# A hybrid retention/HGRN2 decoder layer: four mixing groups first, then three feed-forward groups, nearly all products by a seven-product scheme

## The chip, the cores and the metric

One NeuronCore of a Trainium2 chip runs the whole program. TensorE (PE) multiplies matrices into PSUM; its weight loads are shown as PEld. VectorE (DVE), ScalarE (ACT) and GpSimd (POOL) do elementwise work; SyncE (SP) issues the transfers, which 16 DMA engines carry. The metric is the device time of the program in microseconds (us), as the median of the runs; lower is better.

## What is computed

One layer of a decoder over 2048 prompt tokens and 8 samples of 8 tokens (2112 in all), in float32, with width 1024 and a hidden width of 4096:

```
h = rmsnorm(x, norm_mix_w)
rq, rk, rv, rg, hq, hf, hi, hg = split(h @ w_in, 8)        # 8 parts of 4 heads x 128
o_r = retention(rotary(rq), rotary(rk), rv)                # state S <- g S + k^T v, decay g per head
f = lb + (1 - lb) * sigmoid(hf)
o_h = hgrn2(silu(hq), 1 - f, hi, log f)                    # state S <- diag(f) S + k^T v
o = [head_rmsnorm(o_r) * silu(rg), head_rmsnorm(o_h) * silu(hg)]
x = x + o @ w_out
x = x + square(relu(rmsnorm(x, norm_ffn_w) @ w_up)) @ w_down
y = rmsnorm(x, final_norm_w)
```

The prompt starts from zero states, the samples from given ones. The outputs are y for both and the final states. The two recurrences run over the tokens in order, in chunks of 128 tokens here.

## The kernel before

Activations lie with channels on the 128 partitions and tokens along the free axis. A product of two float32 matrices is made of three TensorE products of rounded parts: each operand is cut in a high part `hi` (a cast on ScalarE) and the rest `lo` (a subtraction on VectorE or GpSimd), and hi*hi + hi*lo + lo*hi are summed in PSUM. So each block of 128 x 128 weights costs three products, each as wide as the tokens that move through it, and a weight tile `raw` of 128 x 1024 is loaded, cast (L277) and subtracted (`second_part`, L292) ahead of its use (`weight`, L252).

The tokens go in three groups: 512 of the prompt; the 64 of the samples and 768 of the prompt; 768 of the prompt. Each goes through the whole layer before the next. Within a group, `mix` (L614) loops over four heads p: `project` (L665) makes six blocks of the input projection through `proj` (L339, products at L352), in pieces of at most 512 tokens, `values` (L708) the two value parts with tokens as the stationary operand (L728), and `mixer` (L829) plans the recurrence: decays in logarithms, scores in chunks on TensorE, states, gates. `residual` (L1181) and `out_proj` (L1345) make the output projection and add x.

The feed-forward of the first group is plain (`up_first`, `down_first`). The other two groups use a scheme of seven products in place of eight for a product of 2 x 2 blocks: sums S1 to S4 of weight quarters A11 to A22 and T1 to T4 of activation quarters B11 to B22 are operands beside the quarters (`PRODUCTS`, `OCTET`), each product is half the group's tokens wide, and results are added on the way out of PSUM (`up`, L1492; `down`, L1579; products at L1176). The weight sums are made once on VectorE while the first group's feed-forward and the second's mixing run (`plan_sums`, L1314), written to DRAM and loaded in both later groups. Input weights are also cut once and kept in DRAM as hi and lo.

The order of the work is written by an agenda that counts ticks: one tick for each step of three products in `proj`, or for two products elsewhere (`tick`, L221). Functions are due at a tick (`later`, `at`), so mixer work is laid between wide products; `side` is a second list, for `plan_sums`. A scheduler then orders each engine's instructions by readiness, with the order of the program as priority, and the engines take their queues in order. Slabs (42 of 832 columns) are the working tiles in SBUF; a tile is used again when its last reader is done. All weight loads go out through SP's queue.

PSUM is split in two tiles of two banks for projections (`pj`) and four of one bank (`mm`).

Of the kernel before, what the change touches and what calls it, by code (L numbers as in the profile page):

```python
# [15 lines left out]
P = 128  # L16
# [12 lines left out]
SLAB = 832  # L29
NSLAB = 42  # L30
NLD = 6
# [5 lines left out]
GROUPS = ((0, 0, 512), (NS, 512, 768), (0, 1280, 768))  # L37
NT = NS + SEQ
WT = 1024
N_IN, N_OUT, N_UP, N_DN = 32, 8, 32, 32  # L40
W_OUT0 = N_IN
W_UP0 = W_OUT0 + N_OUT
W_DN0 = W_UP0 + N_UP
NQ = FF // (4 * P)
NO = NQ // 2

W_UQ0 = W_DN0 + N_DN
W_DQ0 = W_UQ0 + N_UP
NW = W_DQ0 + N_DN

N_MADE = 4

# [10 lines left out]
PLACE = {name: q for q, name in QUARTER.items()}  # L63
# [17 lines left out]
N_ORDER = (0, 1, 4, 5, 2, 3, 6, 7)  # L81

# [63 lines left out]
def in_blocks():  # L146
    for p in range(H):
        if p:
            yield from ((7, p - 1), (3, p - 1))
        yield from ((5, p), (4, p), (0, p), (1, p), ("v", p))  # L150
    yield from ((7, H - 1), (3, H - 1))


def lay_out_weights(w_in, w_out, w_up, w_down):
    w = np.empty((NW, P, WT), np.float32)
    wi = w_in.reshape(KB, P, 8, H, DK)
    i = 0
    for part, p in in_blocks():
        if part != "v":
            w[i] = wi[:, :, part, p].transpose(1, 0, 2).reshape(P, WT)  # L160
            i += 1
            continue
# [6 lines left out]
    for ps in (range(0, H - 1), range(H - 1, H)):  # L169
        bl = [wo[kind, p, :, n] for n in N_ORDER for p in ps for kind in (1, 0)]  # L170
        for j in range(0, len(bl), 8):
            w[i] = np.stack(bl[j:j + 8], 1).reshape(P, WT)
            i += 1
    wu = w_up.reshape(KB, P, FF // P, P)
    for f in range(FF // P):
        w[i] = wu[:, :, f].transpose(1, 0, 2).reshape(P, WT)
        i += 1
    wd = w_down.reshape(8, 4, P, 4, 256)
    for f in range(8):
        for n in range(4):  # L180
            w[i] = wd[f, :, :, n].transpose(1, 0, 2).reshape(P, WT)
            i += 1
# [25 lines left out]
class Kernel:  # L208
# [12 lines left out]
    def tick(self):  # L221
# [4 lines left out]
        self.n_ticks += 1  # L226
        while self.side and self.side[0][0] <= self.n_ticks:
            self.side.popleft()[1]()
# [8 lines left out]
    def get(self, dt=F32):  # L237
        return self.sl.tile([P, SLAB], dt, tag="slab", name="slab")
# [6 lines left out]
    def load(self):  # L245
        return self.ld.tile([P, SLAB], F32, tag="ld", name="ld")
# [5 lines left out]
    def weight(self, i):  # L252
        n = len(self.stream)
        while self.w_next < min(i + 1 + self.ahead, n):
            j = self.w_next
            e = self.stream[j]
            if e[0] == "p":

                self.wts[j] = tuple(self.wp.tile([P, WT], F32R, tag=tag, name=tag) for tag in ("hi", "lo"))
                for part, kept in zip(self.wts[j], self.kept[e[1]]):  # L260
                    self.nc.sync.dma_start(part.bitcast(F32), kept)
                self.w_next += 1
                self.w_load = max(self.w_load, j + 1)
                continue
            while self.w_load <= j or j >= self.n_first and self.w_load <= j + 2 and self.w_load < n:
                if self.stream[self.w_load][0] == "p":
                    break
                k, later = self.w_load, self.w_load >= self.n_first
                raw = self.raws[k] = self.wp.tile([P, WT], F32, tag="sum" if later and k % 3 else "raw", name="raw",
                                                  bufs=4 if later and k % 3 else 2)  # L270
                e = self.stream[k]
# [1532 lines left out]
```

## Time and profile before

| | |
|---|---|
| runs | 2559.78, 2559.78, 2560.04 us; median 2559.78 |
| profiled execution | span 2557.8 us from the first instruction to the last, 2.0 us under the median of the runs |
| TensorE busy | 2527.3 us, 99%, 14681 products |
| VectorE, ScalarE, GpSimd busy | 67%, 46%, 28% |
| moved by DMA | 443 MB, 173 GB/s on the mean |

A row of instruction groups has the line, the engine, the operation, out<-in with shapes, the count, then busy time and the mean of one in ns, then the idle time of the engine before them and what ended it. Mean durations of products overlap each other, since they are pipelined: a pace has to be taken from counts over a stretch. A row of stages has the stretch, its length, and for each engine its busy time and count, then the clock granted to TensorE as a share, the DMA share and GB/s.

### The profile page before, as it was taken

The numbers are of one execution on the slowest core, as the hardware profiler recorded it, in microseconds if no ns is written. First come the engines' busy times: TensorE is split into PE (matmuls) and PEld (weight loads), VectorE is DVE, ScalarE is ACT, GpSimd is POOL, SyncE is SP. The second block draws the span as 40 slices with busy tenths as digits, with TensorE's granted clock in tenths as the row PEclk, the third lists the DMA queues.
The fourth block names the chain that finished last, engine by engine and source line by source line (L and its number), as shares of the span: only waits on it lengthen the run. The fifth ranks groups of instructions, "written<-read, shape, count | busy, mean of one in ns | idle before, by whom it ended". The sixth has DMA issues, their size and how long they took to land. (4 is left out here: it accounts for less than half of the span.)

```text
span 2557.8 us, 37262 instructions
## 1 busy us (share of the span) xinstructions
PE 2527.3 (99%) x14681; PEld 2398.5 (94%) x14681; DVE 1702.4 (67%) x2165; ACT 1172.3 (46%) x1591; POOL 704.8 (28%) x453
## 2 busy tenths in 40 slices
PE   8999999999999999999999999999999999999997
PEld 7888888888999999999999999999999999999997
DVE  6777775556667667664656978775456465559886
ACT  6776532325444444344434544544445264344443
POOL 4333241111324243101222322243134012223222
PEclk9999999999999999999999999999999999999999
DMA  7666854563264564634457545342223325565552
GB/s 265 219 220 223 294 197 172 190 215 125 94 231 152 198 205 173 230 126 165 166 171 258 191 173 170 129 165 93 94 100 112 120 91 179 176 226 186 176 179 83
DMA packets 147391, 443.13 MB, mean 173 GB/s; under 512 B 15120, under 2 KB 37392, under 8 KB 147216
## 3 DMA queue, kind: packets, MB, share of 16 engines
q1 hardware_dynamic: 147072, 440.73, 49.8%
q8 instruction: 116, 1.90, 0.3%
q14 instruction: 59, 0.48, 0.1%
q10 hardware_dynamic: 144, 0.02, 0.0%
HBM read 331.11 MB, written 108.79 MB: 172 GB/s over the span
## 5 line engine op out<-in xcount | busy, mean ns | idle before, releaser
L352 PE MATMUL pj<-slab,hi 128*128 128x416 f32 (+2 forms) x2844 | 739.3, 363 | 7.4 <-ACT hi L277 6.3
L277 ACT CAST hi<-raw 128x1024 fp32r<-128x1024 f32 x330 | 347.7, 1054 | 673.4 <-PE pu L1176 191.5
L352 PEld LDWEIGHTS pj<-slab,hi 128*128 128x128 f32 x2844 | 513.0, 189 | 38.7 <-ACT hi L277 6.3
L292 POOL TENSOR_TENSOR lo<-raw,hi 128x1024 fp32r<-128x1024 f32 x92 | 248.0, 2695 | 849.6 <-ACT hi L277 788.9
L1176 PE MATMUL pd<-slab,hi 128*128 128x416 f32 (+1 forms) x1792 | 469.4, 342 | 5.1 <-DVE slab L1619 3.1
L292 DVE TENSOR_TENSOR lo<-raw,hi 128x1024 fp32r<-128x1024 f32 x238 | 302.0, 1269 | 199.1 <-ACT hi L277 198.6
L352 PE MATMUL pj<-slab,lo 128*128 128x416 f32 (+2 forms) x1422 | 433.6, 363 | 0.0
L1176 PE MATMUL pu<-slab,hi 128*128 128x416 f32 (+1 forms) x1600 | 408.3, 342 | 0.0
L1176 PEld LDWEIGHTS pd<-slab,hi 128*128 128x128 f32 x1792 | 329.6, 188 | 8.7 <-DVE slab L1619 3.7
L1176 PE MATMUL pd<-slab,lo 128*128 128x416 f32 (+1 forms) x896 | 307.8, 344 | 0.0
L1176 PEld LDWEIGHTS pu<-slab,hi 128*128 128x128 f32 x1600 | 294.0, 188 | 1.5
L352 PEld LDWEIGHTS pj<-slab,lo 128*128 128x128 f32 x1422 | 259.5, 188 | 15.4 <-DVE lo L292 0.8
L1176 PE MATMUL pu<-slab,lo 128*128 128x416 f32 (+1 forms) x800 | 264.2, 343 | 0.0
L352 PE MATMUL mm<-slab,hi 128*128 128x512 f32 x740 | 229.6, 390 | 0.0
L728 PE MATMUL pjv<-hi,slab 128*128 128x256 f32 x1088 | 212.4, 287 | 1.3 <-ACT slab L738 1.3
L1375 DVE TENSOR_TENSOR slab<-slab 128x832 fp32r<-128x832 f32 (+1 forms) x144 | 163.0, 1149 | 36.9 <-ACT slab L1371 17.4
L728 PEld LDWEIGHTS pjv<-hi,slab 128*128 128x128 f32 x1088 | 174.3, 190 | 3.7 <-ACT slab L738 2.2
L1371 ACT CAST slab<-slab 128x832 fp32r<-128x832 f32 (+1 forms) x144 | 122.4, 862 | 116.2 <-DVE slab L1382 83.2
L1176 PEld LDWEIGHTS pd<-slab,lo 128*128 128x128 f32 x896 | 168.1, 188 | 0.5
L352 PEld LDWEIGHTS mm<-slab,hi 128*128 128x128 f32 x740 | 138.5, 188 | 29.2 <-ACT slab L1206 0.4
L728 PE MATMUL pjv<-lo,slab 128*128 128x256 f32 x544 | 153.8, 283 | 0.0
L1176 PEld LDWEIGHTS pu<-slab,lo 128*128 128x128 f32 x800 | 149.7, 188 | 0.5
(214 smaller groups left out, 3685.8 us busy)
## 6 DMA issues: line engine op xcount, KB each, us to landing
raw<-w SPq DMA_DIRECT2D x270, 512.0 KB, 4.2
u<-ld SPq DMA_DIRECT2D x32, 416.0 KB, 4.5
slab<-u SPq DMA_DIRECT2D x32, 416.0 KB, 5.6
u<-ld SPq DMA_DIRECT2D x32, 384.0 KB, 4.5
slab<-u SPq DMA_DIRECT2D x32, 384.0 KB, 5.7
ld<-x SPq DMA_DIRECT2D x16, 416.0 KB, 6.1
ld<-x SPq DMA_DIRECT2D x16, 384.0 KB, 4.1
raw<-su1S SPq DMA_DIRECT2D x8, 512.0 KB, 4.3
```

Source lines behind the costliest of these rows:

```text
L277: self.nc.scalar.copy(hi, raw)
L292: eng.tensor_tensor(out=lo, in0=self.second.pop(j), in1=hi.bitcast(F32), op=ALU.subtract)
L352: self.nc.tensor.matmul(pj[:, i, :T2], w, a[:, c0:c1], start=j == 0 and q == 0, stop=j == n - 1 and q == 2)
L728: nc.tensor.matmul(pj[:, i * 256:(i + 1) * 256], a[:, s:s + C], ww, start=kb == 0 and q == 0, stop=kb == KB - 1 and q == 2)
L1176: self.nc.tensor.matmul(*a, **k)
L1371: self.nc.scalar.copy(hi[:, :g.T], B[name][:, :g.T])
L1375: self.nc.vector.tensor_tensor(out=lo[:, :g.T], in0=B[name][:, :g.T], in1=hi.bitcast(F32)[:, :g.T], op=ALU.subtract)
```

## The change

All four groups' mixing runs first, in groups of 512, 512, 512 and 576 tokens (the samples are with the last one). Then the feed-forward runs in three groups of 704, cut without regard to the mixing groups.

- Six of the eight parts of the input projection come as three pairs of parts a head (`PAIRS`). The pairs of the first head are plain in all groups, those of the second head in the first group; the rest takes seven products of half the group's tokens (`two`). Weights come as half units of 512 columns with hi and lo in one tile. Sums are made on GpSimd in the first group that needs them, kept in DRAM as hi and lo and loaded later; raw quarters are loaded and cut anew in each group, their low part on GpSimd. The activations are normalised before the projection, not after it, go through DRAM (`g.td`), and their sums T1 to T4 are made in `plan_sides`.
- Sigmoids of a head are gathered, with one pair of table loads. The score tiles `AT`, `ATs` exist twice, for even and odd heads.
- The output projection is cut in two halves: heads 0 and 1 while mixing (`out_part`), with x added and the result sent to DRAM; heads 2 and 3 at the start of a feed group (`out_proj`). All head outputs go to DRAM (`spill`) and come back (`load_heads`), gathered from the mixing groups that hold the tokens.
- The feed-forward is by seven products throughout. The four weight sums of a set are made on GpSimd for each group (`first_sums`, `last_sum`), in 16 raw tiles; nothing of them is kept. The reciprocal of the mean square in `scale_residual` goes; `guard` adds a term to the last norm in its place.
- The pools are opened one after the other: 62 slabs of 576 columns and eight PSUM tiles of one bank while mixing, then 44 slabs of 704 and four PSUM tiles of two banks.
- A tick is now 704 columns moved through TensorE (`TICK`).

The core of the diff:

```diff
-GROUPS = ((0, 0, 512), (NS, 512, 768), (0, 1280, 768))
+GROUPS = ((0, 0, 512), (0, 512, 512), (0, 1024, 512), (NS, 1536, 512))
+NFG = 3
+NRAW, NSUM, NFRAW = 4, 2, 16
+POOL_PARTS = ("A12", "S1", "S4")
+PAIRS = ((5, 4), (0, 1), (7, 3))
+PLAIN = (0, 1, 2) if STRASSEN_IN else tuple(range(NBP))
+LATE = (3, 4, 5)
+BP_ORDER = (("A11", "B11"), ("S2", "T2"), ("S3", "T3"), ("S1", "T1"), ("A12", "B21"), ("A22", "T4"), ("S4", "B22"))
...
+    def plan_pair(self, i, bp):
+        plain = self.plain(i, bp)
+        for name in BP_PLAIN if plain else [a for a, _ in BP_ORDER]:
+            made = i == 0 if plain else i == (bp in LATE)
+            self.units.append(("made" if made else "raw" if plain or name[0] == "A" else "op", bp, name, i))
...
+    def half_unit(self, j, raw, eng):
+        t = self.wts[j] = self.w_tile()
+        self.nc.scalar.copy(t[:, :HALF], raw)
+        self.second[j] = (raw, t[:, :HALF], t[:, HALF:])
+        self.later_part(j, eng, 2)
...
+        if kind == "op":
+            t = self.wts[j] = self.w_tile()
+            nc.sync.dma_start(t.bitcast(F32), self.kept[e[1:3]])
...
+        elif kind == "raw":
+            self.half_unit(j, self.raws.pop(j), nc.gpsimd)
...
+    def first_sums(self, key):
+        x, eng = self.parts_of[key], self.nc.gpsimd
+        x["S1"], x["S2"] = self.feed_raw(), self.feed_raw()
+        for out, a, op, b in (("S1", "A21", ALU.add, "A22"), ("S2", "S1", ALU.subtract, "A11"),
+                              ("A21", "A11", ALU.subtract, "A21")):
+            eng.tensor_tensor(out=x[out], in0=x[a], in1=x[b], op=op)
+        x["S3"], x["last"] = x["A21"], (x["A11"], x["A12"], x["S2"])
...
+        for i, g in enumerate(gs):
+            self.mix(g, gs[i + 1] if i + 1 < len(gs) else None)
+            self.out_part(g)
...
+        with self.soon():
+            self.load_heads(fs[0], (2, 3))
+            self.flush()
+        for i, g in enumerate(fs):
+            if i:
+                self.finish(fs[i - 1])
+            self.out_proj(g)
+            self.ffn(g, fs[i + 1] if i + 1 < NFG else None)
...
+        def product(ps=None):
+            first = ps is None
+            if first:
+                ps = self.bank()[:, :T2]
+            _, op = next(todo)
+            for kb, (wh, wl) in enumerate(self.operand()):
+                ah, al = self.moving(g, op, kb)
+                for j, (w, a) in enumerate(((wh, ah), (wh, al), (wl, ah))):
+                    self.matmul(ps, w, a, start=first and kb == j == 0, stop=kb == KB // 2 - 1 and j == 2,
+                                skip_group_check=not first)
+            return ps
...
+    def load_head(self, g, p, hd):
+        s = self.get()
+        self.gather(g, s, lambda m: m.od[p, hd])
+        hi, lo = g.oc[p][1 - hd]
+        self.cut(s, hi, lo, g.T, 2)
...
+    def matmul(self, out, w, a, **k):
+        self.nc.tensor.matmul(out, w, a, **k)
+        self.columns += a.shape[-1]
+        while self.columns >= TICK:
+            self.columns -= TICK
             self.tick()
```

More of the change, by code (lines that the diff above doesn't have):

```diff
@@ L621, in mix @@
         prev = None
[L622 removed]
         for p in range(H):
             b = {}
[L625 to L628 removed]
+            gates = self.gates(g, p - 1, prev) if p > 1 else ()
+            if p == H - 1 and nxt is not None:
+                self.norm_squares(nxt)
+            if p == 0 and not g.post:
+                g.h = [g.h_next[kb] for kb in range(KB)]
+                for k in range(2):
+                    self.plan_sides(g, k, 14 + 44 * k, 10)
@@ L1522, in up @@
         nc.scalar.copy(b2(p1), a)
-        b = [self.mm(T2) for _ in range(2)]
-        product(b)
-        for i in range(2):
-            nc.vector.tensor_tensor(out=b2(u2)[:, i], in0=b[i], in1=b2(p1)[:, i], op=ALU.add)
+        b = bank2()
+        product(parts(b))
+        add(u2, b, p1)
         product(parts(a), first=False)
```

1089 lines of the change are left out of this document (586 added, 503 removed).

## The prediction

> **What bounds the kernel now.** I read the page first: the share of each engine, then the slices.
>
> ```profile
> span 2557.8 us, 37262 instructions
> PE 2527.3 (99%) x14681; PEld 2398.5 (94%) x14681; DVE 1702.4 (67%) x2165; ACT 1172.3 (46%) x1591; POOL 704.8 (28%) x453
> PE   8999999999999999999999999999999999999997
> PEclk9999999999999999999999999999999999999999
> ```
>
> TensorE is busy for 99% of the span at its full clock, so the time is a count of products times their pace, and the question is what each width costs. For that I asked for busy time by stage, in stretches where products of one width run alone: all kinds (first four rows below), then the value products by themselves (L728, the last six rows, each one whole run of 84).
>
> ```profile
> core 0: us, PE busy (x) PEld busy (x) DVE busy (x) ACT busy (x) POOL busy (x), PEclk, DMA share, GB/s
> 350.00:600.00 250.00, 250.00 (x1104) 207.01 (x1104) 133.09 (x137) 74.33 (x92) 38.20 (x23) 1.00 0.52 189
> 1150.00:1600.00 450.00, 450.00 (x2385) 445.89 (x2384) 314.41 (x282) 199.71 (x217) 109.70 (x42) 1.00 0.54 185
> 2100.00:2340.00 240.00, 240.00 (x1386) 240.00 (x1385) 144.18 (x140) 110.44 (x123) 68.72 (x25) 1.00 0.59 195
> 50.00:250.00 200.00, 198.51 (x1227) 170.47 (x1227) 148.78 (x280) 140.60 (x231) 69.42 (x71) 1.00 0.66 224
> ...
> 94.34:104.60 10.26, 10.23 (x84) 10.08 (x84) 1.00 0.53 208
> 153.05:163.31 10.26, 10.23 (x84) 10.08 (x84) 1.00 0.60 210
> 680.94:691.20 10.26, 10.24 (x84) 10.04 (x84) 1.00 0.28 102
> 783.08:793.34 10.26, 10.24 (x84) 10.04 (x84) 1.00 0.29 104
> 1679.62:1689.70 10.08, 10.07 (x84) 10.03 (x84) 1.00 0.57 220
> 1767.65:1777.72 10.07, 10.06 (x84) 10.03 (x84) 1.00 0.31 107
> ```
>
> Paces: 512 columns 250/1104 = 226.4 ns, 416 columns 188.7, 384 columns 173.2, 256 columns 10.07/84 = 119.9. The line through 256 and 384 has 0.417 ns a column and about 13 ns a product, and 512 lies on it. So narrow products lose 13 ns each, no more. The line gives 133 ns at 288 columns and 160 ns at 352, the two widths that are new here; 416 lies 2 ns above the line, so 352 is bounded by 160 and 162.
>
> The starts of those runs are also one head apart: 58.7 us in the first group (T=512), 102.1 in the second (832), 88.0 in the third (768). Taking off the wide products of a head (144 of 512 and 96 of 256 columns: 44.1 us; 288 of 416 and 168 of 256: 74.5; 288 of 384 and 144 of 256: 67.2) leaves 14.6, 27.6 and 20.8 us for the mixer's small products, its switches and its waits. Per chunk of 128 tokens that is 3.6 us with four chunks and 3.5 with six: the remainder goes by the chunk, and hardly by the group. The samples add 6.8 us a head.
>
> **The wide products, part by part.** Counts come from the loops, and the answers for three lines over the whole span (projections L352, values L728, seven-product feed-forward L1176) bear out their totals.
>
> ```profile
> 0.00:2557.90 2557.90, 1172.94 (x5376) 968.69 (x5376) 1.00 0.50 173
> ...
> 0.00:2557.90 2557.90, 212.44 (x1632) 202.29 (x1632) 1.00 0.50 173
> ...
> 0.00:2557.90 2557.90, 985.62 (x5424) 977.36 (x5424) 1.00 0.50 173
> ```
>
> Input projection. Before: 24 blocks of 24 products, once for T=512 and twice for each half of the larger groups: 576 x 226.4 + 1152 x 188.7 + 1152 x 173.2 ns = 547 us. After: twelve pairs a group. A plain pair has 48 products as wide as the group, a seven-product pair has 7 x 12 = 84 of half its width. Plain are six pairs in the first group and three in the others: 288 + 144 + 144 = 576 of 512 columns and 288 of 288. Seven-product pairs are 6 + 9 + 9 of 256 columns (2016) and 9 of 288 (756). Sum 576 x 226.4 + 2016 x 119.9 + 1044 x 133 = 511 us: **36 saved**. The columns fall by an eighth in those pairs; 756 products more, at 13 ns, give back 10 us of it.
>
> Output projection: 183 us before and 183 after (288 of 512, 192 of 288, 576 of 352 columns). The values are 17 starts x 4 heads x 24 as before: 0.
>
> Feed-forward. Before: 1536 products of 512 for the first group (plain), 2712 of 416 and 2712 of 384: 1330 us. After: 3 x 2712 of 352: 8136 x 160 = 1302 us. **28 saved**, or 10 at 162 ns.
>
> Mixer: chunks stay 16 and the samples one. The remainders were 14.6 + 27.6 + 20.8 = 63.0 us over a head index; after, four groups of four chunks and the samples give 4 x 14.6 + 6.8 = 65.2, times four heads: **9 more**.
>
> So 2557.8 - 36 - 28 + 9 = 2503 us if nothing new is late.
>
> **What comes to lie beside it, and may be late.** ScalarE, VectorE and GpSimd get other work, and these rows price it (instruction groups of the page; of the last 200 us of down projection; of 1290 to 1340 us, where GpSimd is little disturbed; the DMA issues):
>
> ```profile
> L277 ACT CAST hi<-raw 128x1024 fp32r<-128x1024 f32 x330 | 347.7, 1054 | 673.4 <-PE pu L1176 191.5
> L292 POOL TENSOR_TENSOR lo<-raw,hi 128x1024 fp32r<-128x1024 f32 x92 | 248.0, 2695 | 849.6 <-ACT hi L277 788.9
> ...
> L1375 DVE TENSOR_TENSOR slab<-slab 128x768 fp32r<-128x768 f32 x42 | 45.8, 1107 | 8.7 <-PE pd L1176 7.5 <-ACT slab L1371 0.3 <-issue 0.3
> L1589 DVE TENSOR_TENSOR slab<-pd,slab 128x768 f32<-128x768 f32 x48 | 45.5, 951 | 20.3 <-PE pd L1176 20.2
> L292 DVE TENSOR_TENSOR lo<-raw,hi 128x1024 fp32r<-128x1024 f32 x28 | 36.6, 1307 | 0.1
> ...
> L292 POOL TENSOR_TENSOR lo<-raw,hi 128x1024 fp32r<-128x1024 f32 x5 | 12.0, 2399 | 42.4 <-ACT hi L277 42.4
> ...
> raw<-w SPq DMA_DIRECT2D x270, 512.0 KB, 4.2
> ```
>
> Weight parts in mixing. Each half unit costs ScalarE half of 1054 ns and its low part half of 2695 on GpSimd. A seven-product unit lasts 12 x 120 ns = 1.44 us on TensorE, and five are held ahead: 7.2 us. Copy 0.5 and low part 1.35 leave some 5 us, which hold three other GpSimd instructions of 1.35 in its queue, not four. The ready-made sums come as one 512 KB transfer (4.2 us to landing) in the same 7.2. GpSimd stood at 35% in the 50 to 250 us stretch; 39 to 51 half-unit instructions a group (39 x 1.35 = 53 us in the last two, of some 235) bring it to 60%. I take 3 us; the bounds are 0 and one late part in each of the 33 seven-product pairs, 33 x 1.35 = 45. All issues go through SP's queue, where a raw half that waits for one of its two tiles holds back the operand loads and spills behind it, so those are in the same bound.
>
> The seam. Heads and half-done residuals now go to DRAM and back. Feed group 0 needs tokens 0 to 703, mixed long before, and its 192 output products (31 us) can cover the last mixer's tail. If memory comes free late, a load of 4.2 us and the split into parts stand open, and a spill before it: 0 to 12 us, taken as 3.
>
> Down projection. The four sums of each set move to GpSimd and are made anew for every group. An octet lasts 14 units x 24 x 160 ns = 53.7 us. GpSimd: 8 sums and 5.6 low parts at 2.4 us = 32.6. VectorE at 704 columns: 14 additions from PSUM at 0.88 us (L1589 scaled) = 12.4, and with both inputs in SBUF 22 at 0.88 and 8.4 low parts at 1.22 = 29.7. Alone that fits. What the two do to each other shows where GpSimd was loaded before (timeline of both engines):
>
> ```profile
> 317.86 1.21 DVE L292 TENSOR_TENSOR lo<-raw,hi 128x1024 fp32r<-128x1024 f32 x1
> 319.00 0.68 DVE L1255 TENSOR_TENSOR slab<-slab 128x512 f32<-128x512 f32 x1
> 322.78 1.86 DVE L292 TENSOR_TENSOR lo<-raw,hi 128x1024 fp32r<-128x1024 f32 x1 [2.02 <-ACT hi L277]
> 324.57 1.78 DVE L1255 TENSOR_TENSOR slab<-slab 128x512 f32<-128x512 f32 x1
> 326.27 2.31 DVE L1324 TENSOR_TENSOR raw<-raw 128x1024 f32<-128x1024 f32 x1
> ...
> 319.76 1.30 POOL L1256 TENSOR_TENSOR slab<-slab 128x512 fp32r<-128x512 f32 x1 [2.37 <-DVE slab L1255]
> 321.01 14.89 POOL L1231 TENSOR_TENSOR slab<-slab 128x512 f32<-128x512 f32 x8
> ...
> 1400.00:1450.00 50.00, 50.00 (x267) 49.54 (x266) 48.79 (x46) 26.32 (x29) 14.79 (x5) 1.00 0.62 218
> ```
>
> Side by side, 1.21 becomes 1.86 to 2.31, 0.68 becomes 1.78, and 1.30 becomes 1.86. GpSimd keeps 0.70 of its pace and VectorE about 0.52: together 1.22 of one engine. An octet then needs 12.4 us of additions (GpSimd unhindered), (32.6 - 12.4)/0.70 = 28.9 us side by side, and 29.7 - 15.0 = 14.7 us of VectorE alone: 56.0, over by 2.3, in 12 octets 28 us. The bounds are 0 and 28; the last row (VectorE at 48.8 of 50 us, TensorE still full) speaks for the low end: 4 us.
>
> [...]
>
> Costed at nothing: ACT's table loads, fewer since sigmoids come in batches, with ACT at 70% in the 50 to 250 stretch and the added splits about as long; the sums T of the activations (16 halves and 8 splits, some 15 us of VectorE a group, 74% busy there). Uncovered, they would add their 15 us in three groups, which the upper range holds.
>
> Sum: 2503 + 3 + 3 + 4 = 2513; the runs are 2.0 us above the span (2559.8 to 2557.8): **2515**.
>
> **Rivals.**
> 1. Nothing new is late, and the waits in the remainder shrink, since scores of two heads now have buffers of their own. For it: 200 - 198.5 us without TensorE in the 50 to 250 row is already little, so it can't be much. 2503 + 2 less up to 1 us in 16 head rounds: 2490.
> 2. Weight parts late in mixing: 45 us in place of 3, 2557 at the worst, 2545 in the middle. For it: GpSimd's share nearly doubles; against: the lead of 5 us.
> [...]
>
> **How the numbers follow.** Forecast (2500 to 2535) 45%, first rival 20%, second 20%, third 10%; 5% for several of the upper bounds at once. This kernel's runs tell about 0.2% (5 us) apart from no change. Slower gets the third and part of the second and of the rest: 14%; within 0.2%: 5%; faster: 81%. Range 2468 to 2588: below, the first rival with 352 and 288 columns a little under the line; above, the second rival with 162 ns a product and the 28 us. The forecast's own range is 2500 to 2535.
>
> **What would show it.** Feed-forward at 160 ns a product with TensorE full in the octets; wide products of 256 columns at 120 ns outside the values; head rounds of 55 to 58 us in mixing. Wrong would be: TensorE idle before products that wait for a low part on GpSimd, rounds of over 65 us, VectorE at 100% with gaps between products in the down projection, or more than 15 us open at the seam.

## The result, and the profile after

The changed kernel takes 2876.1 us (median; 2873.5 to 2877.7) against 2559.9 us: a ratio of 1.123, interval 1.122 to 1.125. The forecast was 2515 us, its range ended at 2588. So 316 us were lost where 45 were to be gained.

The page of the changed kernel: span, busy shares, and three rows of the 40 slices.

```profile
span 2873.7 us, 43910 instructions
PE 2578.2 (90%) x16754; PEld 2480.5 (86%) x16754; DVE 2249.8 (78%) x2816; ACT 1324.8 (46%) x2125; POOL 1353.6 (47%) x817
PE   6987789988998899979999888999978889998888
DVE  6877777667576766646879999678899977879997
PEclk8998899999999999999999999999999999999999
```

TensorE is no longer full. Its idle time lies in two places: all through the mixing, and in three valleys in the second half, each where VectorE stands at 9. The busy time by stage (columns: stretch, length, then busy time and count of PE, PEld, DVE, ACT, POOL, the granted clock, the DMA share and GB/s) is read first for mixing and feed-forward (the border is the first product of the feed groups' output projection), then for an up projection, for two of the three down projections, and for a run each of products of 288 and of 256 columns:

```profile
0.00:1289.40 1289.40, 1128.12 (x8014) 1045.33 (x8014) 898.57 (x1694) 649.50 (x1286) 611.50 (x556) 0.95 0.59 200
1289.40:2873.70 1584.30, 1450.09 (x8740) 1435.19 (x8740) 1351.19 (x1122) 675.25 (x839) 742.11 (x261) 0.96 0.38 127
...
1350.00:1400.00 50.00, 50.00 (x315) 50.00 (x314) 38.85 (x31) 27.22 (x35) 24.79 (x8) 1.00 0.36 114
1550.00:1800.00 250.00, 208.88 (x1209) 205.40 (x1208) 235.23 (x177) 92.49 (x108) 141.94 (x49) 0.92 0.36 114
2090.00:2320.00 230.00, 190.64 (x1094) 187.80 (x1093) 221.59 (x160) 82.81 (x97) 139.46 (x47) 0.92 0.32 103
...
965.10:971.21 6.11, 6.11 (x47) 6.11 (x47) 5.37 (x8) 0.71 (x2) 3.14 (x2) 1.00 0.44 152
835.36:841.71 6.35, 6.35 (x55) 6.35 (x54) 5.84 (x9) 4.56 (x8) 3.07 (x2) 1.00 0.93 323
```

The prediction's sum of 2503 us had 1394 us for the feed groups (1302 and 92 of output projection) and so 1109 for all else. Measured are 1584.3 and 1289.4: **190 too many in the feed-forward, 180 in the mixing**. The paces are not to blame where nothing waits: 50/315 gives 159 ns at 352 columns, and the last two rows, from the start of the first product to that of the last, 6.11/46 = 133 ns at 288 and 6.35/53 = 120 ns at 256. (54 of the 55 in the last row are of that width.) In the down projections an octet of 336 products takes 250/1209 x 336 = 69.5 us instead of 53.7.

TensorE's waits in the mixing (first fence) and in the feed-forward (second), as total, times and longest:

```profile
PE mm L663 <- ACT slab L479: 23.6, 6, 9.3
PE po L1377 <- DVE S L1390: 19.8, 11, 5.9
PE pj L1494 <- DVE slab L1012: 17.4, 6, 6.1
```

```profile
PE pj L1494 <- DVE slab L1758: 60.2, 14, 7.1
PE pj L1494 <- ACT slab L1538: 31.2, 6, 6.7
PE pj L1494 <- ACT w L351: 15.2, 3, 5.1
```

In the feed-forward TensorE waits most for VectorE's additions from PSUM (L1758), which free the PSUM tiles. In the mixing no single wait leads; the mixers' small products wait for VectorE and ScalarE, with the wide products queued behind them.

How the two engines run in a down projection shows in a timeline (start, length, both in us; VectorE and GpSimd rows):

```profile
1651.22 2.62 DVE L431 TENSOR_TENSOR w<-raw,w 128x1024 fp32r<-128x1024 f32 x1
...
1652.85 9.23 POOL L397 TENSOR_TENSOR raw<-raw 128x1024 f32<-128x1024 f32 x3
1653.77 3.08 DVE L1549 TENSOR_TENSOR slab<-slab 128x704 f32<-128x704 f32 x1
1656.78 0.88 DVE L1758 TENSOR_TENSOR slab<-pj,slab 128x704 f32<-128x704 f32 x1
...
1657.58 2.29 DVE L1542 TENSOR_TENSOR slab<-slab 128x704 fp32r<-128x704 f32 x1
```

The addition with one input in PSUM takes 0.88 us beside the sums. One of the same size with both inputs in SBUF (L1549, L1542) takes 2.29 or 3.08, where a row of f_memset below has 0.88 for it alone. Three sums on GpSimd take 9.23, 3.08 each, where the prediction's rows have 2.40 for such an instruction: each waits for a VectorE instruction, and that one for the next sum. They take turns.

### The profile page after: what moved, and what is told of

It is laid out like the page before. It is cut to its first block, busy times and chain, and to the rows that moved or that the text cites. A ratio compares the mean times of both kernels' runs of the same rounds, so it can differ in the third digit from the quotient of the medians.

```text
span 2873.7 us, 43910 instructions
## 1 busy us (share of the span) xinstructions
PE 2578.2 (90%) x16754; PEld 2480.5 (86%) x16754; DVE 2249.8 (78%) x2816; ACT 1324.8 (46%) x2125; POOL 1353.6 (47%) x817
## 4 chain that ended last, share of the span: by engine, by line
PE 38%; DVE 18%; issue 4%; DMA 2%; ACT 2%; POOL 0%; SPq 0%; DVEq 0%; ACTq 0%; POOLq 0%
PE pj L1494 37%; DVE slab L1542 5%; DVE slab L1549 4%; DVE w L431 3%; DVE slab L1758 2%; DMA slab<-o 1%; DVE slab L1761 1%; ACT w L351 0%; DMA raw<-w 0%; ACT slab L1538 0%; PE mm L1195 0%; DVE slab L1841 0%; PE mm L1383 0%; PE po L1377 0%; DMA ld<-x 0%
## 5 line engine op out<-in xcount | busy, mean ns | idle before, releaser
L1494 PE MATMUL pj<-slab,w 128*128 128x352 f32 (+3 forms) x12828 | 2145.2, 325 | 167.0 <-DVE slab L1758 60.2
L1494 PEld LDWEIGHTS pj<-slab,w 128*128 128x128 f32 x12828 | 2023.3, 193 | 222.1 <-ACT slab L1538 71.4
L431 POOL TENSOR_TENSOR w<-raw,w 128x512 fp32r<-128x512 f32 (+1 forms) x203 | 384.6, 1898 | 512.1 <-ACT w L345 220.7
L351 ACT CAST w<-raw 128x1024 fp32r<-128x1024 f32 x343 | 359.7, 1049 | 531.7 <-PE pj L1494 499.3
L431 DVE TENSOR_TENSOR w<-raw,w 128x1024 fp32r<-128x1024 f32 (+1 forms) x335 | 497.0, 1488 | 59.2 <-ACT w L351 32.5
L397 POOL TENSOR_TENSOR raw<-raw 128x1024 f32<-128x1024 f32 x135 | 400.3, 2973 | 160.6 <-DVE w L431 109.0
L1542 DVE TENSOR_TENSOR slab<-slab 128x704 fp32r<-128x704 f32 x216 | 309.2, 1451 | 34.4 <-ACT slab L1538 28.0
L404 POOL TENSOR_TENSOR raw<-raw 128x1024 f32<-128x1024 f32 x45 | 127.8, 2839 | 424.0 <-DVE w L431 423.0
L1494 PE MATMUL pj<-w,slab 128*128 128x256 f32 x1632 | 248.6, 302 | 21.3 <-DVE slab L1012 13.7
L1494 PEld LDWEIGHTS pj<-w,slab 128*128 128x128 f32 x1632 | 224.0, 205 | 25.7 <-DVE slab L1012 8.6
L1758 DVE TENSOR_TENSOR slab<-pj,slab 128x704 f32<-128x704 f32 x166 | 145.8, 881 | 52.7 <-PE pj L1494 52.7
L1549 DVE TENSOR_TENSOR slab<-slab 128x704 f32<-128x704 f32 x120 | 181.8, 1530 | 1.2 <-PE pj L1494 1.0
```

What stands on the lines that cost most here:

```text
L351: self.nc.scalar.copy(hi, raw)
L397: eng.tensor_tensor(out=x[out], in0=x[a], in1=x[b], op=op)
L404: self.nc.gpsimd.tensor_tensor(out=x["S4"], in0=a, in1=b, op=ALU.subtract)
L431: eng.tensor_tensor(out=lo, in0=raw, in1=hi.bitcast(F32), op=ALU.subtract)
L1494: self.nc.tensor.matmul(out, w, a, **k)
L1542: self.nc.vector.tensor_tensor(out=lo[:, :g.T], in0=B[name][:, :g.T], in1=hi.bitcast(F32)[:, :g.T], op=ALU.subtract)
```

## The experiments

All times are of the whole kernel. The two columns at the right come from one trace each, cut at the first product of the feed groups' output projection, like the first two rows above; where the code of a stretch was untouched it came out between 1279 and 1290 us (mixing) and between 1584 and 1592 (feed), the slower tick aside.

| run | us | against 2876 | mixing | feed |
|---|---|---|---|---|
| changed kernel | 2876.1 | | 1289.4 | 1584.3 |
| f_nosums | 2738.4 | -138 | 1290.3 | 1448.5 |
| f_memset | 2714.8 | -161 | 1286.0 | 1424.8 |
| f_vector | 2791.1 | -85 | 1289.1 | 1496.7 |
| f_kept | 2768.6 | -108 | 1279.2 | 1483.9 |
| f_copy | 2801.6 | -75 | 1281.0 | 1517.1 |
| m_keep | 2882.0 | +6 | 1291.3 | 1588.3 |
| m_plain | 2794.3 | -82 | 1206.1 | 1588.4 |
| m_tick | 2897.1 | +21 | 1294.3 | 1601.2 |
| m_noT | 2844.1 | -32 | 1252.0 | 1587.8 |
| m_noapply | 2846.8 | -29 | 1252.2 | 1591.7 |
| mg_memset | 2801.8 | -74 | 1207.6 | 1589.6 |
| mx_memset | 2824.6 | -52 | 1227.4 | 1592.3 |
| mf_all | 2615.8 | -260 | 1192.7 | 1424.5 |
| mf_allna | 2593.3 | -283 | 1165.3 | 1426.6 |
| fm_assembled | 2668.3 | -208 | 1204.2 | 1460.4 |

The first set asked what makes the down projections late and what the mixing. In the expectations, P and later E stand for one theory: GpSimd's reads of SBUF keep VectorE from running. Its rivals are told where they stand. The kernels of m_keep, m_plain, m_tick, f_vector, f_kept and fm_assembled compute the whole layer; the others leave a part of it out, or write constants in its place, to see what it costs.

**f_nosums.** The weight sums of the feed-forward are left out.

```diff
     def first_sums(self, key):
-        x, eng = self.parts_of[key], self.nc.gpsimd
...
+        x = self.parts_of[key]
+        x["S1"], x["S2"], x["S3"], x["S4"] = x["A21"], x["A22"], x["A21"], x["A12"]
```

> The four weight sums of each set are left out in all three feed-forward groups: the seven products take raw quarters in their place, so the output is not the reference's; everything else is done. Theory P (GpSimd and VectorE hinder each other, so that VectorE is full in the down projection): the gaps of the down projection go, about 160 us in the three groups, to some 2715 us. Theory W (VectorE has too much work of its own in the down projection): under 30 us, 2850 or more. Theory L (the sums themselves come late from GpSimd's queue): as P here.

Measured 2738.4, ratio 1.070 (1.067 to 1.073). That is 23 us over the 2715 of theories P and L. The sums on GpSimd cost 138 us, though no product waits for one directly.

**f_memset.** GpSimd is kept as busy as before, but with writes only.

```diff
-        for out, a, op, b in (("S1", "A21", ALU.add, "A22"), ("S2", "S1", ALU.subtract, "A11"),
-                              ("A21", "A11", ALU.subtract, "A21")):
-            eng.tensor_tensor(out=x[out], in0=x[a], in1=x[b], op=op)
+        for out in ("S1", "S2", "A21"):
+            for _ in range(3):
+                eng.memset(x[out], 0.01)
```

> Each weight sum of the feed-forward is replaced by three GpSimd memsets into the same tile, so GpSimd stays occupied and the tiles are written at the same places, but nothing is read from SBUF; the output is not the reference's. Theory P, if the hindrance is between instructions that read SBUF: VectorE runs at its undisturbed durations beside them and the time is near that without the sums, 2715 to 2740 us. Theory L (GpSimd's queue is late): no better than the changed kernel if the memsets take as long as the sums, 2840 or more.

Measured 2714.8, ratio 1.061 (1.058 to 1.064). The first down projection of this run, in the stretch quoted above, and its feed-forward as a whole:

```profile
1550.00:1800.00 250.00, 246.02 (x1535) 244.28 (x1535) 214.00 (x233) 118.22 (x149) 141.95 (x112) 1.00 0.45 144
...
1286.00:2710.80 1424.80, 1402.32 (x8740) 1396.70 (x8740) 1069.81 (x1122) 676.66 (x839) 702.06 (x615) 0.99 0.43 142
```

GpSimd is busy for the same 142 of 250 us, and TensorE makes 1535 products in place of 1209, while VectorE, with more to do in that stretch, is busy for less of it. So it isn't GpSimd's queue that is late; it is what GpSimd reads. Feed-forward against feed-forward, 160 us are gone: 112 of waiting (1584.3 - 1450.1 against 1424.8 - 1402.3) and 48 of the same 8740 products running faster. That second part is the granted clock, 0.96 against 0.99 over the feed-forward and 0.92 against 1.00 in the down projection: waits cost again behind their end. The constants also read nothing that they could wait for, so this run by itself takes away more than the hindrance of VectorE; f_copy and f_vector below bear on that. That it beats the run without sums by 24 us is not explained. There, TensorE waits 16 us for the additions from PSUM, against 1.4 here.

**f_copy.** Does it take two inputs on GpSimd's side? Each sum is two copies here (L397 and L405), with one input.

```diff
+        for out, a in (("S1", "A22"), ("S2", "A11"), ("A21", "A12")):
+            for _ in range(2):
+                eng.tensor_copy(x[out], x[a])
```

> Each weight sum of the feed-forward is replaced by two GpSimd copies from one tile to another, so GpSimd reads one SBUF input in place of two (results are wrong). If any read on GpSimd's side excludes VectorE's two-input instructions: the down projections stay late, 2800 us or more, by how long the copies take. If GpSimd must have two inputs as well: like the constants, 2705 to 2745.

Measured 2801.6, ratio 1.094 (1.091 to 1.097): one input is enough. The groups of VectorE's and GpSimd's instructions from 1500 to 2800 us (columns: count, then busy time and mean of one in ns, then idle time before them), of the changed kernel, of f_memset and of f_copy:

```profile
L397 POOL TENSOR_TENSOR raw<-raw 128x1024 f32<-128x1024 f32 x114 | 338.6, 2979 | 107.2 <-DVE w L431 102.1 <-DMA raw<-w 0.3
...
L1542 DVE TENSOR_TENSOR slab<-slab 128x704 fp32r<-128x704 f32 x197 | 284.9, 1468 | 24.0 <-ACT slab L1538 17.8 <-PE pj L1494 5.0
...
L1549 DVE TENSOR_TENSOR slab<-slab 128x704 f32<-128x704 f32 x112 | 172.5, 1557 | 1.2 <-PE pj L1494 1.0
...
L1758 DVE TENSOR_TENSOR slab<-pj,slab 128x704 f32<-128x704 f32 x149 | 131.0, 881 | 44.4 <-PE pj L1494 44.4
```

```profile
L398 POOL MEMSET raw<- 128x1024 f32 x335 | 319.1, 956 | 329.3 <-DMA raw<-w 253.7 <-DVE w L433 62.0
...
L1544 DVE TENSOR_TENSOR slab<-slab 128x704 fp32r<-128x704 f32 x200 | 230.5, 1171 | 34.0 <-ACT slab L1540 20.2 <-PE pj L1496 11.9
...
L1760 DVE TENSOR_TENSOR slab<-pj,slab 128x704 f32<-128x704 f32 x166 | 146.0, 883 | 51.0 <-PE pj L1496 51.0
...
L1551 DVE TENSOR_TENSOR slab<-slab 128x704 f32<-128x704 f32 x112 | 110.3, 1002 | 1.7 <-PE pj L1496 1.5
```

```profile
L397 POOL COPY raw<-raw 128x1024 f32<-128x1024 f32 x221 | 332.5, 1521 | 344.9 <-DMA raw<-w 292.6 <-DVE w L432 43.3 <-issue 3.7
...
L1543 DVE TENSOR_TENSOR slab<-slab 128x704 fp32r<-128x704 f32 x200 | 273.0, 1387 | 21.7 <-ACT slab L1539 18.3 <-PE pj L1495 2.1
...
L1550 DVE TENSOR_TENSOR slab<-slab 128x704 f32<-128x704 f32 x112 | 138.0, 1249 | 0.2
...
L1495 PE MATMUL pj<-slab,w 128*128 128x352 f32 x7363 | 1209.3, 326 | 73.3 <-POOL w L432 34.9 <-DVE slab L1759 15.6 <-ACT w L351 12.5
```

The additions with two SBUF inputs go from means of 1.47 and 1.56 us to 1.17 and 1.00 when GpSimd only writes, and stand at 1.39 and 1.25 in the run with copies. The additions from PSUM take 0.88 us in both of the first two. Single instructions of f_memset show the undisturbed times:

```profile
1599.52 0.88 DVE L1551 TENSOR_TENSOR slab<-slab 128x704 f32<-128x704 f32 x1
...
1608.13 2.99 POOL L398 MEMSET raw<- 128x1024 f32 x3 [3.86 <-DMA raw<-w]
...
1609.27 1.21 DVE L433 TENSOR_TENSOR w<-raw,w 128x1024 fp32r<-128x1024 f32 x1
```

A low part on VectorE takes its 1.21 us while GpSimd writes. What is left over 0.88 in the means of f_memset fits the low parts that GpSimd still makes.

The whole time of f_copy holds a second effect. TensorE waits 34.9 us for GpSimd's own low parts (L432), which it does neither in the changed kernel nor in f_memset. So of the 87 us between f_copy and f_memset, not all is what the copies do to VectorE; the durations show the hindrance, the total does not measure it.

**f_vector.** The sums move to VectorE: more work for the engine that is already full.

```diff
-        x, eng = self.parts_of[key], self.nc.gpsimd
+        x, eng = self.parts_of[key], self.nc.vector
...
-            self.nc.gpsimd.tensor_tensor(out=x["S4"], in0=a, in1=b, op=ALU.subtract)
+            self.nc.vector.tensor_tensor(out=x["S4"], in0=a, in1=b, op=ALU.subtract)
```

> The four weight sums of the feed-forward are made on VectorE instead of GpSimd; everything else is the changed kernel. Theory E (a VectorE instruction with two SBUF inputs and a GpSimd instruction that reads SBUF never run together): a sum costs 1.22 us of VectorE in place of some 2.4 us in which VectorE stands. The kernel without sums had VectorE at about 45 us an octet; with 8 x 1.22 = 9.8 us it has 55 to 57, a little over the 53.7 of the products: 2755 to 2800 us, some 80 to 120 below the changed kernel. Theory V (VectorE has too much work of its own, GpSimd hinders it little): 9.8 us more for the engine that was already full makes it slower than the changed kernel: 2900 us or more.

Measured 2791.1, ratio 1.090 (1.086 to 1.093). Giving VectorE all the sums makes the kernel 85 us faster, which no theory of an engine with too much work of its own allows. A stretch of its first down projection:

```profile
1550.00:1750.00 200.00, 184.91 (x1102) 181.16 (x1101) 194.54 (x182) 84.12 (x100) 58.44 (x20) 0.97 0.38 128
```

An octet takes 200/1102 x 336 = 61.0 us: still late, since VectorE is now full in earnest; 55 to 57 had been expected.

**f_kept.** The sums are made in the first feed group alone, kept in DRAM and loaded in the others, as the kernel before did.

```diff
+    def made_unit(self, key, name, pool):
+        return ("kept", (key[1:], name)) if key[0] and name[0] == "S" else ("x", key, name, pool)
...
-        elif e[0] == "keep":
+        elif e[0] == "keep" or e[0] == "x" and e[1][0] == 0 and e[2][0] == "S":
...
         x, eng = self.parts_of[key], self.nc.gpsimd
+        if key[0]:
+            return
```

> One part of the change undone: the weight sums of the feed-forward are made on GpSimd in the first feed group only, kept in DRAM as high and low part, and loaded in the other two, as the kernel before did. Results are the same. Theory E: without any sums a group of the three gained some 45 us; two groups gain that, and a little more, since the sums' casts and low parts go too: 2761 to 2790 us. If the loads (1 MB for each of the four sums of a set) come late instead, or the hindrance comes from the low parts: 2820 or more.

Measured 2768.6, ratio 1.082 (1.078 to 1.085). First and second down projection:

```profile
1540.00:1740.00 200.00, 175.24 (x1026) 172.60 (x1025) 186.73 (x141) 79.73 (x94) 122.41 (x43) 0.94 0.71 254
2020.00:2240.00 220.00, 216.25 (x1345) 214.59 (x1344) 157.82 (x163) 68.31 (x86) 27.21 (x10) 1.00 0.83 291
```

An octet takes 65.5 us in the first group and 55.0 in the second. The loads, 291 GB/s with the DMA engines 83% busy, come in time.

**m_keep.** Now the mixing. All input weights are loaded in ready parts in the last three groups, so their low parts leave GpSimd (and VectorE).

```diff
-            self.units.append(("made" if made else "raw" if plain or name[0] == "A" else "op", bp, name, i))
+            self.units.append(("made" if made else "op", bp, name, i))
...
-        if e[0] == "made" and e[2][0] == "S":
+        if e[0] == "made" and not (e[3] == 0 and e[1] in LATE):
```

> Mixing alone: all input weight halves, not the sums alone, are kept in DRAM as hi and lo by the group that cuts them first, and loaded by the later groups; 39 to 51 casts on ScalarE and low parts on GpSimd fall away in each of groups 1 to 3, and each raw half (256 KB) becomes a load of 512 KB. Theory P (GpSimd's added work hinders VectorE and makes it late in mixing too): 60 to 100 us less, 2780 to 2815 us. Theory O (the order of the work and VectorE's own added work make the waits in mixing): under 25 us less, 2850 or more. If transfers are the bound, more than before: over 2880.

Measured 2882.0, ratio 1.126 (1.123 to 1.129). GpSimd's busy time in the mixing falls from 611 to 461 us, and nothing is gained. The time lies above the 2880 that had been set for transfers, but the added loads (237 GB/s in place of 200) came in time: TensorE waited 3 us for loaded weights in the mixing. So the weights' low parts are not the main cause. Whether the loads, and the order of the queues, took back a smaller gain isn't shown.

**m_plain.** The input projection is plain throughout.

```diff
-STRASSEN_IN = True
+STRASSEN_IN = False
```

> The input projection is plain in all four mixing groups (no sums of weights or activations there, no additions out of PSUM); the normalised activations no longer go through DRAM. TensorE has 36 us more to do at full pace. Theory P/W (the elementwise work that the seven products bring makes the mixing late): the waits of mixing fall from some 200 to about 60 us, 2760 us in all. Theory O (four groups, their boundaries and the overlapping heads make it late, whatever the projection): 2900 us or more.

Measured 2794.3, ratio 1.092 (1.088 to 1.095): above the 2760 of theory P/W and far below the 2900 of theory O. It is 82 us faster, with products that by the prediction's paces cost 36 us more. The seven-product form of the input projection thus brings some 118 us by its side effects: TensorE's idle time in the mixing falls by 80 us (161 to 81), and its busy time, which should have risen by 36, falls by 3, at a granted clock of 0.97 in place of 0.95.

**m_tick.** More time between the steps of the agenda.

```diff
-TICK = 704
+TICK = 900
```

> A tick is 900 columns of TensorE in place of 704, so that every step of the mixers, the loads and the sums has 28% more time behind the step before it; nothing else changes. Theory C: the waits in mixing fall by a third or more, 2800 to 2840 us. Theory E: the engines have the same work and hinder each other as before, 2860 to 2890, the end of the mixing coming somewhat later.

Measured 2897.1, ratio 1.131 (1.128 to 1.134): above both ranges. The mixing takes 5 us more and the feed-forward, whose steps the tick times too, 17. So the steps are not too close together.

**m_noT.** The activation sums are left out, with their way through DRAM.

```diff
-        if name[0] == "T":
-            return tuple(self.pair(g, s)[:, kb % 2] for s in g.t[name][kb // 2])
+        name = {"T1": "B11", "T2": "B12", "T3": "B21", "T4": "B22"}.get(name, name)
...
-        for i, name in enumerate(("T1", "T3", "T2", "T4")):
-            self.later(when + pace * i, total, name)
-            self.later(when + pace * i + 3, rest, name)
```

> The sums T1 to T4 of the activations in the input projection are left out, with their way through DRAM; activation quarters take their place, so results are wrong. It tells what the sums cost, which the prediction took at nothing. If they are hidden: 2876 within 10 us. If their some 15 us of VectorE a group lie open: about 60 less, 2815. Theory E expects between the two, 2840 to 2865, since VectorE has few free stretches in mixing; theory C expects no more than 15 us, at the group boundaries alone.

Measured 2844.1, ratio 1.111 (1.107 to 1.114): 32 us, within what theory E gave them. They were costed at nothing.

**mg_memset and mx_memset.** GpSimd writes constants in the mixing, first for all its tensor instructions, then for those of mixers and norms alone.

```diff
+class GP:
+    def touch(self, out, n, real, **ins):
+        first = {k: v[:, :1] if k in ("in0", "in1") else v for k, v in ins.items()}
+        real(out=out[:, :1], **first)
+        for _ in range(n):
+            self.nc.gpsimd.memset(out[:, 1:].bitcast(F32), 0.01)
...
-            nc.gpsimd.tensor_tensor(out=D4[:, :, 0, :], in0=mid, in1=B4[:, :, 0, :], op=ALU.subtract)
+            GP(nc).tensor_tensor(out=D4[:, :, 0, :], in0=mid, in1=B4[:, :, 0, :], op=ALU.subtract)
```

> In the mixing groups every tensor instruction on GpSimd works only on the first column (or first block) of its tile and then writes constants to the rest three times, which takes GpSimd about as long but reads nothing; results are wrong by that, the feed-forward is the changed kernel's. Theory E (the exclusion of VectorE and GpSimd also makes the mixing late): some 8 us in each 50 us of VectorE come free and most waits of TensorE go: mixing 80 to 130 us shorter, 2750 to 2800. Theory C (in mixing the steps stand too close behind one another, whatever the engines' pace): less than 25 us shorter, 2850 or more.

> As the run in which GpSimd wrote constants in mixing, but only for the mixers' and norms' own steps; the weights' sums and low parts in mixing are real again (results are wrong by the constants). If it is the mixers' GpSimd steps that hinder VectorE where it matters, at least 50 of the 74 us stay: 2795 to 2826. If it is the weights' sums and low parts, at most 25: 2850 or more. The run that loaded ready-made low parts in three groups gained nothing, which speaks for the first.

Measured 2801.8, ratio 1.094 (1.091 to 1.097), and 2824.6, ratio 1.104 (1.100 to 1.107). The first is 2 us above its range, the second within. With GpSimd busy for longer than before (745 us in the mixing, 611 in the changed kernel) but only writing, 74 us go, 52 of them by the mixers' and norms' own steps. A stretch of the changed kernel shows how (VectorE, GpSimd and TensorE rows):

```profile
183.54 0.68 DVE L431 TENSOR_TENSOR w<-raw,w 128x512 fp32r<-128x512 f32 x1
184.05 1.33 POOL L1013 TENSOR_TENSOR slab<-slab 128x512 f32<-128x512 f32 x1 [2.77 <-ACT slab L940]
184.15 1.78 DVE L1012 TENSOR_TENSOR slab<-slab 128x512 f32<-128x512 f32 x1
...
185.34 1.71 POOL L1202 TENSOR_TENSOR slab<-slab 128x512 f32<-128x512 f32 x1
...
185.85 1.75 DVE L1014 TENSOR_TENSOR slab<-slab 128x512 f32<-128x512 f32 x1
187.01 1.71 POOL L1013 TENSOR_TENSOR slab<-slab 128x512 f32<-128x512 f32 x1
187.52 3.45 DVE L1156 TENSOR_TENSOR_SCAN slab<-reset,slab 128x128 f32<-128x128 f32 x4
...
191.67 0.33 DVE L1390 SCALAR_TENSOR_TENSOR S<-S,slab,mm 128x128 f32<-128x128 f32 x1
191.80 0.80 PE L1377 MATMUL po<-slab,S 128*128 128x128 f32 x2 [5.87 <-DVE S L1390]
```

An instruction of 0.68 us takes 1.75 behind each GpSimd one, a state update (L1390, 0.3 us) stands behind the lot, and TensorE waits 5.87 us for it with the wide products behind. The weights' instructions matter less: they make the other 23 us of the 74, and m_keep, which took 150 us of them away, gained nothing.

**m_noapply.** Two of the three groups that follow another take the first one's normalised activations.

```diff
+            same = nxt is not None and nxt.T == g.T
...
-                if nxt is not None:
+                if same:
+                    nxt.h_next, nxt.td = dict(enumerate(g.h)), g.td
+                    self.later(2, self.tables, nxt)
+                elif nxt is not None:
                     self.norm_apply(nxt)
```

> The second and third mixing group take the first group's normalised activations as their own, so at two of the three group boundaries nothing is loaded, squared, scaled, cast and written for the next group (results are wrong). If that chain, which stands in ScalarE's and VectorE's queues ahead of the last head's steps and waits for its loads, makes the boundaries late: 25 to 45 us less, 2831 to 2851. If the boundaries are late by the mixers' own tail: 2860 or more.

Measured 2846.8, ratio 1.112 (1.109 to 1.114): 29 us. The boundary in the changed kernel:

```profile
341.61 0.75 DVE L785 SCALAR_TENSOR_TENSOR slab<-slab,vec 128x512 f32<-128x512 f32 x1 [1.30 <-DMA slab<-x]
...
342.39 0.62 ACT L788 CAST slab<-slab 128x512 fp32r<-128x512 f32 x1 [2.54 <-DVE slab L785]
...
342.91 0.61 ACT L479 CAST slab<-slab 128x512 fp32r<-128x512 f32 x1
...
343.58 0.58 PE L663 MATMUL mm<-slab,ones_r 128*128 128x256 f32 x1 [9.34 <-ACT slab L479]
```

The next group's scaling (L785) waits for each load of x, its cast (L788) waits on ScalarE for the scaling, and the last head's cast (L479) stands behind those in ScalarE's queue. TensorE waits 9.34 us. The run takes the whole chain away, loads and VectorE's steps included, so it doesn't tell how much of the 29 us is the order in ScalarE's queue.

**mf_all and mf_allna.** Three of the leave-outs together (mg_memset, m_noT, f_memset), then m_noapply with them.

> Three of the leave-outs at once: GpSimd writes constants in mixing and in place of the feed-forward's sums, and the sums T are left out (results are wrong). If the three causes are separate, their gains of 74, 32 and 161 us add up: 2609 us. If the sums T were late mostly because VectorE stood, the two of mixing overlap: 2625 to 2645. Under 2590 would mean that one covered another, and that only what is left, about 75 us, stands against the forecast of 2515.

> All leave-outs at once: constants on GpSimd in mixing and for the feed-forward's sums, no sums T, and the second and third mixing group take the first group's normalised activations (results are wrong). If the next group's normalisation makes the boundaries late in its own right: 29 us less than the 2616 without it, 2580 to 2595. If that gain was the exclusion's and the sums' in another place: 2605 or more. What stands above 2515 then is the mixing's remainder, which the prediction set at 9 us over before.

Measured 2615.8, ratio 1.022 (1.019 to 1.025), and 2593.3, ratio 1.012 (1.010 to 1.015). The first is 7 us from the sum of the parts, the second shows 22 of the boundaries' 29. The mixing of the second run:

```profile
0.00:1165.30 1165.30, 1089.12 (x8010) 1019.62 (x8010) 651.04 (x1551) 626.33 (x1227) 737.30 (x2124) 0.97 0.59 199
```

Against the 1109 us of the sum 56 are left, with TensorE idle for 76 and the clock at 0.97. Their cause stays open.

**fm_assembled.** What of this can be had with nothing left out: plain input projection, sums on VectorE, made once and kept.

> Results are the same as the changed kernel's: the input projection is plain (82 us less when alone), and the feed-forward's sums are made once, on VectorE, kept in DRAM and loaded in the second and third group (107 us less when alone and made on GpSimd; a third of 85 us more on VectorE). Added up: 2876 - 82 - 107 - 28 = 2659 us, so still some 100 us slower than the kernel before. If the two halves of the kernel shared one cause, it would be over 2690.

Measured 2668.3, ratio 1.042 (1.039 to 1.045), 9 us over the sum of the parts. It is 208 us better than the change and still slower than the kernel before.

## Why the prediction was wrong, by its own steps

- **Counts and paces** held: 120, 133 and 159 ns against 120, 133 and 160. The two terms they carry, 36 and 28 us saved, are products' time; waits ate them.
- **Down projection, 4 us (0 to 28).** The step that failed is "GpSimd keeps 0.70 of its pace and VectorE about 0.52: together 1.22 of one engine". The two shares came from different instructions. The 0.70 is a mean over eight of GpSimd's (14.89 us), and VectorE stood idle for 2.02 us beside the first of them. Taken turn by turn, the prediction's own rows show hardly any sharing: 0.68 + 1.30 = 1.98 us of work in 1.78, and 1.21 (a low part, of the size of L1324's sums) + 1.30 = 2.51 us in 2.31, which is 1.09 to 1.11 of one engine. After the change it is 2.40 + 0.88 = 3.28 us in 3.08, 1.06. With 1.11 the prediction's octet would have been 12.4 + (20.2 + 29.7)/1.11 = 57.4 us, with 1.06 59.5: 44 to 69 us in twelve, outside the bound of 28. Measured are 69.5 us an octet, and 160 us of the feed-forward that go when GpSimd stops reading for the sums.
- **"The last row (VectorE at 48.8 of 50 us, TensorE still full) speaks for the low end"** was a misreading: in it GpSimd was busy for 14.8 of 50 us, so it could not tell what 28 would do.
- **The third rival** had the direction and was given 10%. What the runs show: beside constants a low part on VectorE keeps its 1.21 us, beside copies and sums the two-input additions are longer (means of 1.39 and 1.47 us against 1.17), and those with an input in PSUM keep their 0.88 beside all three. If VectorE's 29.7 us with two SBUF inputs and GpSimd's 32.6, both from the prediction's rows, never overlap, an octet takes 62.3 us in place of 53.7, and twelve lose 103. This estimate is near the 112 us of waiting that go in f_memset; the other 48 of the 160 are products that ran at a lower clock. It supposes that one of the two engines always works, and in the groups above GpSimd's sums stood idle for 102 us behind VectorE's low parts (L431): each engine was late for the other. How much of the waiting this coupling adds is not shown.
- **The clock** was taken at 1.00 throughout. In the stretch of 250 us, 1209 products at 159 ns are 192 us, and TensorE was busy for 209: 17 us. Eight of the waits there take 4.8 us on the mean, the longest 7.1. Behind one of them, 3.86 us long and over at 1577.14, the next 3 us hold ten products at half the clock (columns: PE busy and count, granted clock, DMA share, GB/s):

```profile
1577.00:1580.00 3.00, 2.86 (x10) 0.50 0.00 0
```

  In the 3 us after that there are 20, at 0.98. Behind the other seven of the eight, of 3.29 to 7.07 us, the next 3 us hold ten or eleven products at 0.50 to 0.54; behind a wait of 1.80 us, over at 1588.58, they hold 19 at 1.00. Over this stretch the mean granted clock is 0.92, and it is 1.00 in f_memset, where the waits are gone.
- **Sums T, costed at nothing:** 32 us. The prediction's price for them uncovered, 15 us in three groups, was a fair bound.
- **Mixer, 9 us more.** This carried over the first group's remainder of 14.6 us a head round, with its few waits, into rounds in which VectorE and GpSimd both have more to do. The runs showed 52 us by the turns of the mixers' and norms' own steps in its place. The boundaries, 22 to 29 us, were no term at all: that scaling for the next group stands ahead of the last head in ScalarE's queue was to be seen in the order of the code.
- **Weight parts in mixing, 3 us (0 to 45).** The size is within the bound, by another mechanism. The term was for parts that come late, and TensorE waited for none on GpSimd. But constants in place of the weights' sums and low parts gained 23 us (2824.6 - 2801.8, a difference of two runs that are each known to some 8 us).
- **The seam, 3 us (0 to 12),** held: TensorE is idle for 6.6 of the 12 us around the border (1282 to 1294).
- Of the signs that were to show it wrong, VectorE full with gaps between products in the down projections came about. So, by an estimate, did rounds of over 65 us: the 180 us too many over 16 head rounds are 11 each on top of 55 to 58. TensorE did not wait for GpSimd's low parts themselves, but for what VectorE had to put off.

Of the 361 us between 2876 and 2515, then, 161 go with the reads for GpSimd's sums in the feed-forward (138 when the sums are left out), 74 with GpSimd's reads in the mixing, 32 with the sums T and some 22 with the boundaries. With all four out of the way 78 remain (2593 against 2515). Against the sum of 2503, which holds nothing for late work, the same trace is 89 us over, 56 in the mixing and 33 in the feed-forward; the cause of these is open.

## What to carry to other kernels

Before work is moved to GpSimd beside a busy VectorE, add up GpSimd's reading instructions and VectorE's two-SBUF-input instructions as if one engine did both, and leave out the additions with an input in PSUM (0.88 us beside sums, copies and constants alike) and GpSimd's constants. Here that sum gave 103 us where 160 were lost, so take it as a floor. A GpSimd sum of 2.40 us that displaces VectorE cost more than the 1.22 us of doing it there (f_vector), and making it once and loading it, with its cast and low part, cost less than either (f_kept). Read the sharing from pairs (one instruction of each engine in one turn), never from two means. A profile with TensorE at 99% says what products cost and nothing of what added elementwise work will cost. Waits of 3.3 to 7.1 us cost twice here: behind each of the eight in the stretch above the granted clock was 0.50 to 0.54 for 3 us.

## What the runs showed of the hardware

- VectorE and GpSimd took turns, an instruction each: 3.08 us for 2.40 and 0.88. With an addition from PSUM beside it (0.89 us, at 1379.53 in the changed kernel) a sum on GpSimd took 2.41, at 1377.91. GpSimd's writes (constants, 0.96 us on the mean for 128x1024) did not hinder VectorE: 1.21 us for a low part beside three that took 2.99. Its one-input copies, 1.52 us each on the mean, did (means of 1.39 and 1.25 us for VectorE's additions, against 1.17 and 1.00 beside constants). VectorE's scans were slow there as well: four of L1156 take 3.45 us beside GpSimd in the stretch above, and 1.36 at 273.67 us of the same trace, where GpSimd stands idle.
- The granted clock was 0.50 to 0.54 in the 3 us behind each of eight waits of 3.29 to 7.07 us, and 1.00 behind one of 1.80 (changed kernel, 1550 to 1800 us).
- The feed-forward ran 24 us faster with GpSimd writing constants than with those instructions left out. This was not expected, and its cause is open.
